# Second LayerNorm's scale and bias: spread over the partitions by TensorE from 16 columns, in place of a load into all partitions

## The chip, the cores and the metric

The kernel runs on one core of a Trainium2 chip. The metric is the device time of one execution in microseconds (us). The kernel before takes 1108.0 us as the median of three runs (1106.22 to 1109.04).

The core has five engines that take their instructions in order and meet at semaphores: TensorE (PE in the profile; its weight loads are the rows PEld), VectorE (DVE), ScalarE (ACT), GpSimd (POOL) and SyncE (SP), which here issues nearly all transfers. SBUF is the on-chip memory of 128 partitions, PSUM holds the matmul results.

## The reference, cut to what matters

One layer of a decoder with 256 tokens of 1024 features, all float32: four kinds of token mixer, a LayerNorm, a mixture of 32 experts of which each token takes four, and a second LayerNorm. The change concerns only the scale `ln2_g` and the bias `ln2_b` of the last line, 1024 numbers each, the same for all tokens.

```python
mix = token_mixers(x, ...)
x = _layernorm(DEEPNORM_ALPHA * x + mix, ln1_g[l], ln1_b[l])
ffn = moe_ffn(x, router_w[l], router_b[l], w_gu[l], b_gu[l], w_down[l], b_down[l])
x = _layernorm(DEEPNORM_ALPHA * x + ffn, ln2_g[l], ln2_b[l])

def _layernorm(x, g, b):
    mu = jnp.mean(xf, axis=-1, keepdims=True)
    var = jnp.mean(jnp.square(xf - mu), axis=-1, keepdims=True)
    y = (xf - mu) * lax.rsqrt(var + LN_EPS)
    return (y * g + b)
```

## The kernel before, in words

The front part (projections, attention, convolution, first LayerNorm, router) takes about the first 195 us. The rest is a loop over 32 places. The experts are ranked by the number of their tokens, a table gives each place its rank, and each place works on one expert; places 29 to 31 (`TAIL` = 3) are run only if their expert has tokens at all, and their weights are only then loaded (`loads`, behind a test of the count). In the run shown, place 29 is worked on, and places 30 and 31 are not.

The weights of a place are 12 chunks of 1 MiB (128 partitions of 2048 float32): chunks 0 to 7 for the gate and up projection (`up`, L1085), chunks 8 to 11 for the down projection (`down`, L1141). SP issues them in order of use into a ring of 19 slots of that size (tiles `w`, `wx`, `res`), each as soon as the slot's former user has given it back (`released`). TensorE waits in `up` and `down` for the semaphore of each slot. For a place with at most 32 tokens TensorE runs 8 matmul records of 128x512 per chunk in `up` and 16 of 128x256 in `down`.

Between `up` and `down` of a place stand: `act` (VectorE and ScalarE: clamp, sigmoid, products, L1100 to L1109), then on TensorE what the place has to do for others (the gather of a later batch of tokens, the scatter of an earlier batch, L1235, the gates' transposes, L1224, and in place 17 `b_down`, L1254 and L1265), then `h_trans` (two transposes, L1118), ScalarE's copy of them (L1122), the bias of the next place (L1073) and `down`. Places share batches: places 25 to 28 (ranks 16, 20, 24 and 28) are one batch, and place 29 is the first of the last batch, so that in place 29 TensorE scatters the results of places 25 to 28 (L1235) between `up` and `h_trans`. The results of the last batch are scattered after the loop, and then the second LayerNorm and the output follow.

The scale and the bias of the second LayerNorm need every partition to hold the same 2048 numbers. They lie in one ring slot, `g2b2`: SP issues a transfer from one row of `rows`, read 128 times, into all partitions (L1507), after the loads of place 28 and ahead of those of place 29. VectorE waits for it at the end (L1532) and uses it in L1534 and L1540.

```python
for e in range(1, E - TAIL):
    load(e, expert(e))
released(X, g2b2_before)
X.dma_start(g2b2, A["rows"][1:2].to_broadcast([128, SLOT])).then_inc(slot_sem[id(g2b2)], 16)
loads(E - TAIL)
```

The order of the work on each engine is written out by hand in `program`, which is run once for each engine; `take` waits for a semaphore and counts it down.

Of the kernel before, what the change touches and what calls it, by code (L numbers as in the profile page):

```python
# [27 lines left out]
AF = mybir.ActivationFunctionType  # L28
OP = mybir.AluOpType
# [12 lines left out]
SLOT = 2048  # L42
# [14 lines left out]
def _cols(c):  # L57
    if len(c) == 2:
# [7 lines left out]


_STAY = [("ident", 128), ("ones", 128), ("strict", 128), ("iota", 128), ("krow", 32), ("kcol", 2), ("sigma", 32),
         ("rep", 128), ("qmask", 4), ("half", 1), ("g1", 8), ("b1", 8)]
_FIRST = [("tri", 128), ("tri1", 128), ("causal", 256), ("hmask", 2), ("fb", 4), ("rb", 32), ("lam", 128), ("dng", 1),  # L70
          ("cw", 62), ("cb", 2), ("clg", 2), ("clb", 2), ("rw", 256)]
PK, PKW = {}, []
# [32 lines left out]
def layout(x, rel_bias, w_in, forget_b, diff_lambda, diff_norm_g, conv_w, conv_b, conv_ln_g, conv_ln_b,  # L105
           w_out, ln1_g, ln1_b, router_w, router_b, w_gu, b_gu, w_down, b_down, ln2_g, ln2_b):
    f = np.float32
    A = {}
    A["xt"] = np.ascontiguousarray(x[0].T.reshape(8, 128, L).transpose(1, 0, 2))
    A["xs"] = np.ascontiguousarray(x[0].reshape(2, 128, D).transpose(1, 0, 2))  # L110
    for i, c in enumerate(CHUNKS):
        w = np.concatenate([w_in[0][:, o:o + n] for o, n in _cols(c)], axis=1)
        A[f"wi{i}"] = np.ascontiguousarray(w.reshape(8, 128, CW[i]).transpose(1, 0, 2)).reshape(128, 8 * CW[i])
    wo = w_out[0].reshape(4, 2, 128, D)[[1, 2, 3, 0]].transpose(0, 2, 1, 3)
    A["wo"] = np.ascontiguousarray(wo).reshape(4, 128, SLOT)


    we = np.empty((E, 12, 128, SLOT), f)
    we[:, 0:8].reshape(E, 8, 128, 4, 2, 256)[...] = (
        w_gu[0].reshape(E, 8, 128, 4, 256, 2).transpose(0, 1, 2, 3, 5, 4))  # L120
    we[:, 8:12].reshape(E, 2, 2, 128, 2, D)[...] = w_down[0].reshape(E, 2, 2, 2, 128, D).transpose(0, 3, 1, 4, 2, 5)
    A["we"] = we
    A["bg"] = np.ascontiguousarray(b_gu[0].reshape(E, 4, 256, 2).transpose(1, 0, 3, 2)).reshape(128, 512)
    A["bd"] = np.ascontiguousarray(b_down[0].reshape(E, 4, 256).transpose(1, 0, 2)).reshape(128, 256)
    A["rows"] = np.stack([np.concatenate([g[0], b[0]]) for g, b in ((ln1_g, ln1_b), (ln2_g, ln2_b))])
    i = np.arange(128)
    P = {}
    P["ident"] = (i[:, None] == i[None]).astype(f)
    P["tri"] = (i[:, None] <= i[None]).astype(f)
    P["strict"] = (i[:, None] < i[None]).astype(f)  # L130
    P["iota"] = np.broadcast_to(np.arange(1, 129, dtype=f), (128, 128))
    k = np.arange(L)
    P["causal"] = np.where(k[None] <= i[:, None] + 128, 0.0, NEG).astype(f)
    P["ones"] = P["tri1"] = np.ones((128, 128), f)
    e = np.arange(E)
    key = np.where(e < 1, 1e5, -e)
    P["krow"] = np.broadcast_to(key, (128, E))
    P["kcol"] = np.stack([key, e], axis=1)[i % E]
    P["sigma"] = np.broadcast_to(SIGMA, (128, E))
    P["rep"] = (i[:, None] % E == i[None] % E).astype(f)  # L140
    P["qmask"] = (i[:, None] // 32 == np.arange(4)[None]).astype(f)
    P["half"] = np.full((128, 1), -0.5)
    P["hmask"] = (i[:, None] // 64 == np.arange(2)[None]).astype(f)
    P["fb"] = np.broadcast_to(forget_b, (128, 4))
    P["rb"] = np.broadcast_to(router_b, (128, 32))
    P["lam"] = np.broadcast_to(diff_lambda.reshape(1, 128), (128, 128))
    P["dng"] = np.tile(diff_norm_g[0], 2)[:, None]
    P["cw"] = conv_w[0].T.reshape(2, 128, 31).transpose(1, 0, 2).reshape(128, 62)
    for n, a in (("cb", conv_b), ("clg", conv_ln_g), ("clb", conv_ln_b)):
        P[n] = a[0].reshape(2, 128).T  # L150
    P["g1"] = ln1_g[0].reshape(8, 128).T
    P["b1"] = ln1_b[0].reshape(8, 128).T
    P["rw"] = router_w[0].reshape(8, 128, 32).transpose(1, 0, 2).reshape(128, 256)
    for n, l in (("pk0", _STAY), ("pk1", _FIRST)):
        A[n] = np.ascontiguousarray(np.concatenate([np.asarray(P[m], f) for m, _ in l], axis=1))
    dist = i[:, None] + 128 - k[None]
    t5 = rel_bias[_buckets()[np.maximum(dist, 0)]]
    t5 = np.where((dist >= 0)[..., None], t5, f(NEG)).astype(f)
    A["t5"] = np.ascontiguousarray(t5.transpose(0, 2, 1))
    return A  # L160


def body(ctx, tc, nc, A, out):
# [746 lines left out]
    for e in range(E):  # L910
        for c in range(12):
            t, before = queue.pop(0)
            n_used[id(t)] += e > 0
            slots[e, c] = t, before, n_used[id(t)]
            queue.append((t, (e, c)))
            if (e, c) == (0, 3):
                queue.append((rest, "rest"))
        if e == E - TAIL - 1:

            g2b2, g2b2_before = queue.pop(0)  # L920
            n_used[id(g2b2)] += 1
            g2b2_n = n_used[id(g2b2)]

    def sem(name, n=None):
        if n is None:
# [5 lines left out]
    FREE, READY, READYA, HT = sem("free", 8), sem("ready", 8), sem("readya", 8), sem("ht", 8)  # L931

    REL, REL11 = sem("rel"), sem("rel11")
    GC, SG, HH, VV = sem("gc"), sem("sg"), sem("hh"), sem("vv")
    PP, PPX, PGR, PGRX, YX, GT, SQ = [sem(n) for n in ("pp", "ppx", "pgr", "pgrx", "yx", "gt", "sq")]
    SEL, ACC, FIN, RS, RSD, OUT, DONE = [sem(n) for n in ("sel", "acc", "fin", "rs", "rsd", "out", "done")]

    def take(X, s, n=1):
        X.wait_ge(s, n).then_inc(s, -n)  # L939
# [21 lines left out]
    def program(X, kind):  # L961
# [309 lines left out]
        def one_hot_x(e, b):  # L1271
# [3 lines left out]
                                    op0=OP.add, op1=OP.is_equal)  # L1275
            return j

        def gather_x(e, b=0):

            if t_ and (b == 0 and HOME[e] == 4):  # L1280
                take(X, PPX)
            if HOME[e] + 4 * b < NPASS[e] and not s_:
                with more(e, HOME[e] + 4 * b):
                    if v_ and (b or HOME[e] < 4):
                        one_hot_x(e, b).then_inc(PPX)
                    if t_ and (b or HOME[e] < 4):
                        take(X, PPX)
                    for k0 in (0, 4):
                        gather(Px, XGx[b], k0, 6 + k0 // 4)
                    gather_x(e, b + 1)  # L1290
# [70 lines left out]
        def passes(e, end):  # L1361
# [42 lines left out]
            if not many:  # L1404
                scatter_before(e)
                gates_of(e)
                gather_next(e, 0)
                if h < 4:
                    gather_next(e, 4)
                if four(e + 1):  # L1410
                    gather_x(e + 1)
                if e == B_DOWN:
                    b_down()
            h_trans(e, 0)
            if not many and h == 4 and t_:
                take(X, PGRX)
# [20 lines left out]
            if many:  # L1437
                if e + 1 < E:
                    bias(e + 1, 0)
                gates_xT(e)  # L1440
                for k0 in (0, 4):
                    gather_next(e, k0)
                scatter_x(e)
                if four(e + 1):
                    gates_x(e + 1, 0)
                    gather_x(e + 1)
                if e == B_DOWN:
                    b_down()

        def places(first):  # L1450

# [36 lines left out]
        if kind == "SP":  # L1488
            def load(e, x, cs=range(12)):
                for c in cs:  # L1490
                    t, before, _ = slots[e, c]
                    released(X, before)
                    X.dma_start(t, A["we"][ds(x, 1), c].rearrange("o p n -> p (o n)")).then_inc(slot_sem[id(t)], 16)

            def expert(e):
                return X.value_load(eid[:, e:e + 1], min_val=0, max_val=E - 1)

            def loads(e):
                with X.If(X.value_load(cnt[:, e:e + 1], min_val=0, max_val=L) > 0):
                    load(e, expert(e))  # L1500
                    if e + 1 < E:
                        loads(e + 1)

            for e in range(1, E - TAIL):
                load(e, expert(e))
            released(X, g2b2_before)
            X.dma_start(g2b2, A["rows"][1:2].to_broadcast([128, SLOT])).then_inc(slot_sem[id(g2b2)], 16)  # L1507
            loads(E - TAIL)


# [18 lines left out]

        pieces = [(0, 0, D), (1, 0, D // 2), (1, D // 2, D)]  # L1530
        if v_:
            X.wait_ge(slot_sem[id(g2b2)], 16 * g2b2_n)  # L1532
            for tb in range(2):
                X.scalar_tensor_tensor(acc[:, tb], acc[:, tb], mv[:, tb, 0:1], g2, op0=OP.subtract, op1=OP.mult)  # L1534
                X.drain()  # L1535
                X.wait_ge(RSD, tb + 1)
                for t, c0, c1 in pieces:
                    if t == tb:
                        o = acc[:, tb, c0:c1]
                        X.scalar_tensor_tensor(o, o, mv[:, tb, 1:2], b2[:, c0:c1], op0=OP.mult, op1=OP.add).then_inc(OUT)  # L1540
# [43 lines left out]
```

## Time and profile before

| what | value |
|---|---|
| three runs, median (lowest to highest) | 1108.0 us (1106.22 to 1109.04) |
| profiled execution, its own time | 1105.45 us |
| its span, first to last instruction | 1103.7 us |
| TensorE busy | 925.4 us, 84% of the span |
| VectorE, ScalarE, GpSimd busy | 368.1, 173.5, 111.6 us |
| moved by DMA | 403.84 MB, mean 366 GB/s |
| mean granted TensorE clock | 0.904 |

The profiled execution is 2.55 us (0.23%) under the median of the runs. Its time is 1.75 us longer than its span. TensorE's busy share contains stretches at a lower clock, and it is an average over a front part that computes and a loop that mostly waits for weights; which of the two ends last in a stretch is read from that stretch.

### The profile page before, as it was taken

To read this page: it belongs to the slowest core of one execution; us is meant where nothing else is said; L and a number is where in the kernel's file an instruction comes from. 1 tells how busy PE (TensorE), PEld (TensorE's weight loads), DVE (VectorE), ACT (ScalarE), POOL (GpSimd) and SP (SyncE) were. 2 spreads that over 40 slices of the span, in tenths; PEclk is the share of its full clock that TensorE was granted. 3 is DMA by queue.
4 is the path that set the end of the run, shared out by engine and by line. 5 is a ranking of instruction groups with operands and counts; after the bars stand their busy time and mean duration, and the time that the engine had idled before them with its cause. 6 is when DMAs were issued, how large, how long until landed. Compare 5 with 4: busy or idle time off the path is not lost. (4 is left out here: it accounts for less than half of the span.)

```text
span 1103.7 us, 21204 instructions
## 1 busy us (share of the span) xinstructions
PE 925.4 (84%) x8340; PEld 479.9 (43%) x8340; DVE 368.1 (33%) x896; ACT 173.5 (16%) x371; POOL 111.6 (10%) x98
## 2 busy tenths in 40 slices
PE   9887898997799979877799986678999999776672
PEld 8786685453232536322245542132554544322121
DVE  4899655332113223211132331111332333211014
ACT  5525440210001201100011110000110111100000
POOL 2695613000000000000000000000000000000000
PEclk9898898999799999977899998779999999978667
DMA  9635356899999649999999999999999999999981
GB/s 372 247 140 204 115 201 281 355 377 427 426 426 425 245 185 424 425 427 427 425 426 425 425 426 426 426 426 426 425 426 424 425 426 425 425 426 427 426 375 46
DMA packets 57002, 403.84 MB, mean 366 GB/s; under 512 B 6320, under 2 KB 6448, under 8 KB 8368
## 3 DMA queue, kind: packets, MB, share of 16 engines
q1 hardware_dynamic: 56592, 400.98, 87.1%
q8 instruction: 84, 1.38, 0.5%
q10 hardware_dynamic: 288, 1.18, 0.3%
q14 instruction: 38, 0.31, 0.1%
HBM read 401.08 MB, written 1.05 MB: 364 GB/s over the span
## 5 line engine op out<-in xcount | busy, mean ns | idle before, releaser
L1085 PE MATMUL moe<-w,XG 128*32 128x512 f32 x2672 | 354.3, 658 | 84.8 <-DMA w<-in_we_dram 83.0
L1085 PEld LDWEIGHTS moe<-w,XG 128*32 128x32 f32 x2672 | 81.3, 114 | 325.5 <-DMA w<-in_we_dram 186.3
L1141 PE MATMUL moe<-w,hT 128*32 128x256 f32 x2880 | 174.9, 392 | 14.9 <-DMA w<-in_we_dram 10.5
L1100 DVE TENSOR_SCALAR gc<-moe 128x256 f32<-128x256 f32 x49 | 20.8, 425 | 418.3 <-DVEq L939 418.3
L1141 PEld LDWEIGHTS moe<-w,hT 128*32 128x32 f32 x2880 | 95.7, 113 | 88.2 <-issue 22.8
L1109 ACT ACTIVATE h<-gc 128x256 f32<-128x256 f32 x49 | 20.4, 416 | 490.7 <-ACTq L939 490.7
L1486 POOL CAST sel<-sel_q 128x128 fp32r<-128x128 f32 x31 | 9.3, 304 | 821.4 <-PE moe L1085 821.4
L1160 DVE COPY ys<-moe 32x256 f32<-32x256 f32 x94 | 39.5, 421 | 155.1 <-DVEq L939 154.0
L1160 ACT ACTIVATE ys<-moe 32x256 f32<-32x256 f32 x94 | 35.2, 374 | 184.4 <-ACTq L939 183.8
L858 PEld LDWEIGHTS moe<-P,z 128*128 128x128 f32 x448 | 56.7, 207 | 15.6 <-issue 15.5
L858 PE MATMUL moe<-P,z 128*128 128x128 f32 x448 | 60.6, 295 | 0.6 <-PEq L939 0.6
L1235 PE MATMUL moe<-ys,pgT 128*128 128x256 f32 x224 | 54.2, 387 | 4.7 <-PEq L939 3.0
L864 DVE TENSOR_SCALAR XG<-moe,pk 128x128 f32<-128x128 f32 x112 | 38.3, 405 | 50.5 <-DVEq L939 50.0
L262 PE MATMUL pj<-s,h 128*128 128x256 f32 (+1 forms) x272 | 51.5, 292 | 2.1 <-ACT sv L316 2.1
L1235 PEld LDWEIGHTS moe<-ys,pgT 128*128 128x128 f32 x224 | 40.4, 190 | 19.6 <-issue 15.3
L262 PEld LDWEIGHTS pj<-s,h 128*128 128x128 f32 (+1 forms) x272 | 43.6, 196 | 2.9 <-ACT sv L316 2.4
L1073 PE MATMUL moe<-bg,sel 128*128 128x512 f32 x100 | 38.3, 466 | 5.4 <-PEq L939 5.3
L1242 DVE TENSOR_TENSOR acc<-acc,moe 128x512 f32<-128x512 f32 x60 | 39.0, 684 | 9.6 <-DVEq L939 9.3
L262 PE MATMUL pj<-s,l 128*128 128x256 f32 (+1 forms) x136 | 39.5, 290 | 0.7 <-DVE l L279 0.7
L279 POOL TENSOR_TENSOR l<-w,h 128x2048 fp32r<-128x2048 f32 x5 | 30.2, 6068 | 15.4 <-ACT h L274 15.4
L1118 PE MATMUL moe<-pk,h 128*128 128x128 f32 x98 | 21.3, 302 | 12.1 <-PEq L939 12.1
L274 ACT ACTIVATE h<-w 128x2048 fp32r<-128x2048 f32 (+1 forms) x15 | 27.2, 1829 | 4.9 <-DVE l L279 3.4
(284 smaller groups left out, 854.0 us busy)
## 6 DMA issues: line engine op xcount, KB each, us to landing
w<-in_we_dram SPq DMA_DIRECT2D x323, 1024.0 KB, 26.2
wx<-in_we_dram SPq DMA_DIRECT2D x19, 1024.0 KB, 26.6
res<-in_we_dram SPq DMA_DIRECT2D x18, 1024.0 KB, 26.4
w<-in_wi_dram SPq DMA_DIRECT2D x11, 1024.0 KB, 17.3
w<-in_wo_dram SPq DMA_DIRECT2D x4, 1024.0 KB, 5.9
xt<-in_xt_dram SPq DMA_DIRECT2D x4, 256.0 KB, 4.9
w<-in_wi_dram SPq DMA_DIRECT2D x4, 256.0 KB, 5.0
t<-in_t_dram SPq DMA_DIRECT2D x1, 1024.0 KB, 15.6
```

Source lines behind the costliest of these rows:

```text
L262: T.matmul(o, R(l[x]), R(r[y]), start=first and i == 0, stop=last and i == 2)
L274: S.activation(R(view(hi[c][0], c)), view(tiles[c], c), AF.Copy)
L279: eng.tensor_tensor(R(W[c][1]), view(tiles[c], c), W[c][0], op=OP.subtract)
L858: i = X.matmul(p[:, a], z[:, tb, k * 128:k * 128 + 128], P[:, tb], start=tb == 0, stop=tb == 1)
L864: i = X.tensor_scalar(XG[:, k], p[:, a], par("g1")[:, k:k + 1], par("b1")[:, k:k + 1], op0=OP.mult, op1=OP.add)
L1073: X.matmul(pb_[b], R(sels[e % 3]), R(w), start=i == 0, stop=False, skip_group_check=True)
L1085: i = X.matmul(gu[32 * q:32 * q + 32], xg(e, p, k), w[:, q], start=False, stop=k == 7, skip_group_check=True)
L1118: i = X.transpose(q[:, j], hs[p % 2][:, j * 128:j * 128 + 128], ident)
L1141: i = X.matmul(y[o:o + 32], hT8[:, p, j, 32 * q:32 * q + 32], w[:, n * 256:n * 256 + 256], start=(j == 0 and q == 0), stop=(j == 1 and q = ...
L1160: i = X.tensor_copy(dst[o:o + 32, c], y[o:o + 32]) if v_ else X.activation(dst[o:o + 32, c], y[o:o + 32], AF.Copy)
L1235: i = X.matmul(p[:, n * 256:n * 256 + 256], g[:, 2 * (2 * m + n) + tb], y[:, 2 * m + n], start=True, stop=True, skip_group_check=True)
L1242: X.tensor_tensor(o, o, p, op=OP.add).then_inc(FREE[b], 2)
```

## The change

The 2048 numbers come in as 16 columns of a parameter tile (`gb2`: column k holds 128 of them, one on each partition), with the transfer that loads the tile anyway: that one grows from 727 to 743 columns. The transfer of `g2b2` from `rows` is gone, and the slot is still taken out of the ring. A new function `rows2` fills it in place 28, in four rounds of 512 numbers: VectorE multiplies the identity by four of the columns (a 128x512 tile `PGx`, four diagonals), TensorE multiplies a matrix of ones by that tile (each row of the result holds the 512 numbers), and ScalarE copies the result from PSUM into the slot. VectorE may write the next diagonals when ScalarE has seen the matmul end (`DF`). VectorE's wait before the last LayerNorm is for `GB`, which ScalarE raises after the fourth copy.

```diff
-         ("rep", 128), ("qmask", 4), ("half", 1), ("g1", 8), ("b1", 8)]
+         ("rep", 128), ("qmask", 4), ("half", 1), ("g1", 8), ("b1", 8), ("gb2", 16)]
...
-    A["rows"] = np.stack([np.concatenate([g[0], b[0]]) for g, b in ((ln1_g, ln1_b), (ln2_g, ln2_b))])
+    A["rows"] = np.concatenate([ln1_g[0], ln1_b[0]])[None]
...
+    P["gb2"] = np.concatenate([ln2_g[0].reshape(8, 128), ln2_b[0].reshape(8, 128)]).T
...
             g2b2, g2b2_before = queue.pop(0)
-            n_used[id(g2b2)] += 1
-            g2b2_n = n_used[id(g2b2)]
...
+    DD, DF, GB = sem("dd"), sem("df"), sem("gb")
...
+        def rows2():
+
+            if s_:
+                released(X, g2b2_before)
+            for r in range(4):
+                b = 5 + r % 3
+                if v_:
+                    if r:
+                        take(X, DF)
+                    X.tensor_tensor(PGx.rearrange("p t r a b -> p (t r) (a b)"), ident[:, None].to_broadcast([128, 4, 128]),
+                                    par("gb2")[:, 4 * r:4 * r + 4, None].to_broadcast([128, 4, 128]), op=OP.mult).then_inc(DD)
+                if t_:
+                    take(X, DD)
+                    take(X, FREE[b], 2)
+                    X.matmul(pb_[b], par("ones"), PGx.rearrange("p t r a b -> p (t r a b)"), start=True,
+                             stop=True).then_inc(READYA[b])
+                if s_:
+                    take(X, READYA[b])
+                    if r < 3:
+                        X.sem_inc(DF, 1)
+                    X.activation(g2b2[:, 512 * r:512 * r + 512], pb_[b], AF.Copy).then_inc(FREE[b], 2)
+            if s_:
+                X.drain().then_inc(GB)
...
                 if e == B_DOWN:
                     b_down()
+                if e == E - TAIL - 1:
+                    rows2()
             h_trans(e, 0)
...
-            released(X, g2b2_before)
-            X.dma_start(g2b2, A["rows"][1:2].to_broadcast([128, SLOT])).then_inc(slot_sem[id(g2b2)], 16)
             loads(E - TAIL)
...
-            X.wait_ge(slot_sem[id(g2b2)], 16 * g2b2_n)
+            X.wait_ge(GB, 1)
```

The call of `rows2` stands a second time in the form of place 28 for more than 32 tokens, which the run shown does not take.

TensorE's instructions of place 28 before: the last chunks of `up` (L1085), the two transposes (L1118), the bias of place 29 (L1073), `down` (L1141).

```order
L1085 MATMUL moe<-w_1027,XG_1585 32x512 x4
L1085 MATMUL moe<-w_1029,XG_1585 32x512 x4
L1118 MATMUL moe<-pk_66,h_1595 128x128 x2
L1073 MATMUL moe<-bg_67,sel_1600 128x512
L1073 MATMUL moe<-bg_68,sel_1600 128x512
L1141 MATMUL moe<-w_1152,hT_1576 32x256 x8
L1141 MATMUL moe<-res_1317,hT_1576 32x256 x8
```

The same place after; L1292 is the new matmul (`PGx` the diagonals, `pk` the tile with the matrix of ones).

```order
L1085 MATMUL moe<-w_1027,XG_1585 32x512 x4
L1085 MATMUL moe<-w_1029,XG_1585 32x512 x4
L1292 MATMUL moe<-PGx,pk_66 128x512 x4
L1118 MATMUL moe<-pk_66,h_1595 128x128 x2
L1073 MATMUL moe<-bg_67,sel_1600 128x512
L1073 MATMUL moe<-bg_68,sel_1600 128x512
L1141 MATMUL moe<-w_1152,hT_1576 32x256 x8
```

The four matmuls stand between the last chunk of `up` and the transposes, and everything of TensorE behind them keeps its order.

ScalarE's instructions of the same place after: the sigmoid (L1109), the four new copies into the slot (L1298, tile `w_1158`), the copy of the transposes (L1122), its half of the results of `down` (L1160).

```order
L977 COMPARE_AND_BRANCH
L1109 ACTIVATE h_1595<-gc 128x256
L1298 ACTIVATE w_1158<-moe 128x512 x4
L1122 ACTIVATE hT_1576<-moe 128x256
L1160 ACTIVATE ys<-moe 32x256 x2
```

Before, L1122 follows L1109 at once; VectorE has its four products (128x512) at the same place, behind the product that ends `act` (L1106).

SP's transfers before, from the last two chunks of place 28 to the first of place 29.

```order
L1493 DMA w_1154<-in_we_dram 128x2048
L1493 ISA
L1493 DMA w_1156<-in_we_dram 128x2048
L1507 DMA w_1158<-in_rows_dram 128x2048
L1499 TENSOR_LOAD cnt
L1499 ISA x2
L1499 COMPARE_AND_BRANCH
L1496 TENSOR_LOAD eid
L1496 ISA x2
L1493 ISA
L1493 DMA w_1434<-in_we_dram 128x2048
```

After, the row with `in_rows_dram` is missing, and no other row of SP's moves.

## Rows read from the trace of the kernel before

**Rows 1.** The page: bandwidth in 40 slices of the span, wait for weights in `up`, transfers

```profile
GB/s 372 247 140 204 115 201 281 355 377 427 426 426 425 245 185 424 425 427 427 425 426 425 425 426 426 426 426 426 425 426 424 425 426 425 425 426 427 426 375 46
...
L1085 PE MATMUL moe<-w,XG 128*32 128x512 f32 x2672 | 354.3, 658 | 84.8 <-DMA w<-in_we_dram 83.0
...
w<-in_we_dram SPq DMA_DIRECT2D x323, 1024.0 KB, 26.2
```

**Rows 2.** Stretches: from:to, its length, busy us of each engine, PEclk, DMA share, GB/s

```profile
1018.00:1037.40 19.40, 13.02 (x64) 1.48 (x64) 0.74 (x2) 0.59 (x2) 0.29 (x1) 0.68 1.01 426
1037.40:1047.00 9.60, 6.04 (x68) 2.88 (x68) 2.09 (x6) 1.37 (x4) 0.00 (x0) 0.71 1.01 428
...
1050.00:1062.00 12.00, 8.61 (x40) 0.92 (x40) 0.00 (x0) 0.00 (x0) 0.00 (x0) 0.64 1.01 427
1062.00:1070.30 8.30, 5.73 (x24) 0.60 (x24) 0.00 (x0) 0.00 (x0) 0.00 (x0) 0.50 0.91 385
1070.30:1083.00 12.70, 9.81 (x99) 7.29 (x96) 4.95 (x10) 2.52 (x6) 0.00 (x0) 1.00 0.28 118
```

**Rows 3.** Timeline of places 28 and 29, all engines: start, length, instruction, idle before and releaser

```profile
1018.27 6.17 SPq L1507 DMA_DIRECT2D w<-in_rows_dram  x1
...
1039.46 0.42 DVE L1106 TENSOR_TENSOR h<-h,moe 128x256 f32<-128x256 f32 x1 [0.51 <-DVEq L939]
...
1040.02 0.66 PE L1118 MATMUL moe<-pk,h 128*128 128x128 f32 x2 [2.69 <-PEq L939]
...
1040.82 0.38 ACT L1122 ACTIVATE hT<-moe 128x256 f32<-128x256 f32 x1 [2.24 <-ACTq L939]
...
1045.22 1.07 PE L1141 MATMUL moe<-w,hT 128*32 128x256 f32 x16 [0.22 <-DMA w<-in_we_dram]
...
1050.08 1.93 PE L1085 MATMUL moe<-w,XG 128*32 128x512 f32 x8 [3.80 <-DMA w<-in_we_dram]
...
1059.90 1.82 PE L1085 MATMUL moe<-w,XG 128*32 128x512 f32 x8 [1.28 <-DMA w<-in_we_dram]
...
1063.57 1.94 PE L1085 MATMUL moe<-w,XG 128*32 128x512 f32 x8 [1.86 <-DMA w<-in_we_dram]
...
1066.01 1.93 PE L1085 MATMUL moe<-w,XG 128*32 128x512 f32 x8 [0.50 <-DMA w<-in_we_dram]
...
1068.44 1.94 PE L1085 MATMUL moe<-w,XG 128*32 128x512 f32 x8 [0.50 <-DMA w<-in_we_dram]
...
1070.31 4.10 PE L1235 MATMUL moe<-ys,pgT 128*128 128x256 f32 x16
```

**Rows 4.** Lines by form, whole span: nearest forms to the new copy and product

```profile
L1228 ACT ACTIVATE pgT<-moe 128x512 f32<-128x512 f32 x28 | 15.3, 595 | 44.0 <-ACTq L939 44.0
...
L258 DVE TENSOR_TENSOR s<-xt,s 128x1024 fp32r<-128x1024 f32 x2 | 2.4, 1224 | 8.2 <-ACT s L257 8.2
```

**Rows 5.** Timeline of place 17 around its `b_down`: VectorE's last product, then TensorE

```profile
710.74 0.42 DVE L1106 TENSOR_TENSOR h<-h,moe 128x256 f32<-128x256 f32 x1
...
720.96 0.69 PE L1118 MATMUL moe<-pk,h 128*128 128x128 f32 x2
...
722.43 1.94 PE L1141 MATMUL moe<-res,hT 128*32 128x256 f32 x16
724.14 3.47 PE L1141 MATMUL moe<-w,hT 128*32 128x256 f32 x48
727.61 5.36 PE L1085 MATMUL moe<-w,XG 128*32 128x512 f32 x48
734.34 1.07 PE L1085 MATMUL moe<-w,XG 128*32 128x512 f32 x8 [1.37 <-DMA w<-in_we_dram]
736.77 1.06 PE L1085 MATMUL moe<-w,XG 128*32 128x512 f32 x8 [1.37 <-DMA w<-in_we_dram]
```

**Rows 6.** Timeline of an earlier batch change, TensorE

```profile
946.90 1.06 PE L1085 MATMUL moe<-res,XG 128*32 128x512 f32 x8 [1.38 <-DMA res<-in_we_dram]
947.89 4.10 PE L1235 MATMUL moe<-ys,pgT 128*128 128x256 f32 x16
```

More of the change, by code (lines that the diff above doesn't have):

```diff
@@ L1448, in passes @@
                     b_down()
+                if e == E - TAIL - 1:
+                    rows2()
         def places(first):
```

## The prediction

> **What bounds the kernel now.** First the page's bandwidth line [rows 1]: from about the tenth slice nearly every slice stands at 424 to 427 GB/s, two stretches apart, until the last but one; and TensorE's matmuls of `up` have 84.8 us of idle time before them, 83.0 of it put down to transfers of weights. So in the loop the transfers set the pace, although TensorE is the busiest engine. Then the stretches around places 28 and 29 [rows 2]: 426 to 428 GB/s at a DMA share of 1.01 up to 1062 us, so no byte can arrive earlier there unless another byte goes. Then the timeline [rows 3]. TensorE starts the last chunk of place 28 at 1045.22, just after it came (0.22 us idle), and the first chunk of place 29 at 1050.08, after 3.80 us idle. That is 4.86 us for two transfers, the one of the LayerNorm's rows (SP issued it at 1018.27) and chunk 0 of place 29: 2.43 us each. Chunk 7 starts at 1068.44 (0.50 us idle before it, for its transfer). From there TensorE waits for no transfer any more: the scatter of the last full batch follows at 1070.31, then `down`, the last scatter, the LayerNorm and the output. I take 1070.31 to the end of the span at 1103.7 (33.4 us) as a fixed tail, and ask when its first instruction can start.
>
> **The removed transfer.** One transfer of 1 MiB leaves a saturated queue. All 12 chunks of place 29 come behind it, so each lands one step earlier: 2.43 us from the timeline [rows 3]; 1.049 MB at 427 GB/s [rows 2] is 2.46, the same. Chunk 7 is then there at 1068.44 - 2.43 = 1066.01. SP's issue of the removed transfer took 6.17 us [rows 3], but a transfer of weights lands 26.2 us after its issue in the median [rows 1], so some ten are queued, and the issue itself sets nothing. The ring slot is still taken, and no load of place 29 needs a slot that is given back later than chunk 5 of place 28, which TensorE reads before the new work. The new work can therefore not hold up a load. This term: -2.43 us. The 16 columns in the parameter tile are 8 KB, 0.02 us at 427 GB/s, in the front part; the test of `GB` in place of the slot's semaphore costs nothing, since the slot is full by about 1053 and read only behind the scatter of 1070.31.
>
> The Trainium skill ("DMA: Bandwidth & Descriptors", section "Where 436 GB/s comes from") says that for loads from HBM the HBM side binds at about 358 GB/s per core. By that page 1.049 MB would be an estimated 2.93 us, and the forecast 0.5 us lower. The rows measure 427 GB/s, and the measurement decides.
>
> **The added work.** In place 28 the last product of `act` ends at 1039.46 + 0.42 = 1039.88, and TensorE starts the transposes 0.14 us later, at 1040.02 [rows 3]. Now four rounds stand between them, each a chain of VectorE, TensorE, ScalarE and back. No row shows these forms, so by the nearest:
> - the product of 128x512 on VectorE: half of the 1.224 us of 128x1024 is 0.61 [rows 4]; I take 0.65.
> - the matmul: the trace gives two records for each float32 matmul, and 16 records of 256 columns take 4.10 us in the scatter at the full clock of 1.00 [rows 2, 3], 0.256 each. Two records of 512 columns are 4 x 0.256 = 1.03 us at 2.4 GHz, and twice that, 2.05, at 1.2 GHz.
> - a hand-over from engine to engine: 0.14 (VectorE to TensorE, above; TensorE to ScalarE too, 1040.02 + 0.66 to 1040.82 [rows 3]). Three per round, since VectorE's next product waits until ScalarE has seen the matmul end.
> - ScalarE's copy, 0.595 [rows 4], lies beside the next product. The fourth one stands ahead of ScalarE's copy of the transposes: up to 0.3 us.
>
> One round is 0.65 + 1.03 + 3 x 0.14 = 2.10 us at the full clock and 3.12 at half. The first matmul can start at 1040.67 and the transposes after three rounds and one matmul: 1040.67 + 6.30 + 1.03 = 1048.0, or 1040.67 + 9.36 + 2.05 = 1052.1. So TensorE is held 8.0 to 12.1 us, the largest cost of the change. Queued behind it are the transposes, the bias of place 29 and `down` of place 28; ScalarE's and VectorE's parts of the results of `down` wait with them. VectorE and ScalarE have nothing else to do there (2.09 and 1.37 us busy in 9.6 [rows 2]).
>
> **What hides it.** Place 17 shows the same thing with `b_down` [rows 5]: the last product ends at 711.16 and the transposes start at 720.96, a hold of 9.8 us with TensorE at half clock (0.69 us for two transposes). From there 6.65 us pass until `up` of the next place starts at 727.61. Its first six chunks had come meanwhile and are done in 5.36 us, 0.89 each. By 734.34 TensorE waits for a transfer again. With these two durations `up` of place 29 starts between 1048.0 + 6.65 = 1054.7 and 1052.1 + 6.65 = 1058.7, plus up to 0.3. Six chunks later it is 1060.0 to 1064.4. Chunk 6 lands at 1066.01 - 2.43 = 1063.58 and is done by 1065.3 at the latest, and chunk 7 comes at 1066.01. TensorE has caught up 0.7 us before it or more. If `up` started later than 1066.01 - 7 x 0.89 = 1059.8, the delay would begin to show one to one.
>
> **The clock behind it.** In place 29 the clock was low before (0.64, then 0.50 [rows 2]) and chunk 7 took 1.94 us, so the scatter started 1.87 us after it [rows 3]. After catching up, TensorE was at the full clock: in place 17 the two chunks behind the dense stretch take 1.07 and 1.06 us [rows 5], and where a batch change followed one, the scatter starts 0.99 us after the last chunk of 1.06 [rows 6]. I expect this for place 29 too, which gives 0.88 us more.
>
> **The sum**, against the profiled execution: 1105.45 - 2.43 - 0.88 = 1102.1 us. That execution is 2.55 us under the median of the runs, so the forecast for a median is 1108.0 - 3.31 = 1104.7 us.
>
> **Rivals.**
> 1. Only the transfer counts: TensorE has fallen back to 1.2 GHz by chunk 7, or chunks 8 to 11 come so late that `down` waits. 1105.45 - 2.43 = 1103.0, as a median 1105.6. For it: with waits between the chunks the clock does fall (0.68, 0.64 [rows 2]). Against: the first two chunks after catching up were fast in place 17.
> 2. The time is given back: place 29 lands no earlier. For it: chunk 5 of place 29 came 3.67 us after chunk 4 (1059.90 to 1063.57 [rows 3]), 1.24 more than a step, while the share fell to 0.91 and the rate to 385 GB/s [rows 2]; something other than the bytes in the queue held it, and could take the rest too. Against: the step of the removed transfer is there to be seen at full rate. Price: 0, a median of 1108.0.
> 3. Slower: TensorE stays at 1.2 GHz from the first round through `up` of place 29. Transposes at 1052.1; 1.47 us later `down` (720.96 to 722.43 [rows 5]), four chunks at 1.71 (722.43 to 724.14), so `up` from 1060.4; eight chunks at 2 x 0.89 = 1.79 end at 1074.7, 4.4 us after 1070.31. 1109.9, as a median 1112.4. It decides when `up` starts at half clock later than 1070.31 - 14.3 = 1056.0. Against: in place 17 the first chunk of `down` took 1.94, but the next three together 3.47, and then 0.89 per chunk: back to back work brought the clock up.
>
> The Trainium skill speaks for the third ("TensorE: Matmul & The Clock Gate", section "HAM oscillation — how this bites in real kernels"): bursts of matmuls between waits can each start throttled, over and over. By that rule alone the four rounds and what follows run at half clock and the third rival's time comes out. Place 17 agrees with the throttled start and not with its lasting.
>
> **How the numbers follow.** Forecast 0.52, first rival 0.22, second 0.12, third 0.10, and 0.04 for still larger gains. A median of three scatters by an estimated 1.2 us, since the runs shown reach from 1.8 under to 1.0 over theirs. What a measurement of this kernel can tell from no change is about 0.3%, 3.3 us: below 1104.7 is faster, above 1111.3 slower. The forecast lies on that edge and gives half of its chance to faster (0.26), the first rival a third (0.07), the second 0.02, the rest 0.03: 0.38. Slower: 0.08 of the third rival and 0.02 of mishaps in the others: 0.10. Same: 0.52. The forecast's own range is 1103.4 to 1106.0. The range reaches down to 1101.8, for runs as quick as the profiled execution, and up to 1109.2, the second rival with its scatter; beyond it lie the third rival and little else.
>
> **What would show it.** In the profile after: no transfer from `rows`; four matmul pairs in place 28 with 2 to 3 us between their starts; the transposes of place 28 between 1048 and 1053; hardly a wait before the first chunks of place 29 and a wait for a transfer before its chunk 7, which starts near 1066.0 and takes 1.07; the scatter at about 1067.0 and the tail behind it 33.4 us long, as before. A chunk 7 of 1.9 us means the first rival; one that starts at 1068 after a wait, the second; one without a wait before it, after 1066, the third. A tail of another length would make the argument wrong where I looked least.

## The result, and the profile after

The change made the kernel slower: 1116.58 us as the median of four runs (1115.9 to 1119.42) against 1108.3 us of four runs before. The recorded ratio is 1.0095, with a 95% interval of 1.0069 to 1.0121; the plain quotient of the two medians is 1.0075, inside that interval. The forecast was 1104.7 us, 3.6 us faster by this median of before; the result lies above the range.

The first view to read is the page's line of bandwidth, in 40 slices of the span, of the kernel after.

```profile
GB/s 366 248 128 213 113 200 300 343 381 421 420 420 420 244 181 419 420 421 420 420 420 419 419 420 420 421 421 419 419 420 417 420 420 418 421 420 421 420 366 45
```

Before, the slices of the loop stand at 424 to 427 [rows 1]; now they stand at 417 to 421, from the tenth slice on, that is from about 250 us, some 800 us ahead of the place that was changed. The stretches of the kernel after say the same (from:to, length, busy us of PE, PEld, DVE, ACT and POOL, PEclk, DMA share, GB/s); the single line below them is the kernel before:

```profile
420.00:520.00 100.00, 81.07 (x779) 37.17 (x777) 24.50 (x64) 10.05 (x25) 1.45 (x5) 0.89 1.01 420
...
640.00:760.00 120.00, 88.38 (x702) 36.68 (x700) 25.61 (x70) 8.70 (x22) 1.20 (x4) 0.82 1.01 420
...
860.00:962.00 102.00, 98.78 (x1043) 47.47 (x1036) 31.71 (x81) 13.23 (x33) 0.94 (x3) 0.98 1.01 419
```

```profile
860.00:962.00 102.00, 95.50 (x1040) 49.31 (x1036) 34.12 (x85) 14.91 (x37) 0.94 (x3) 1.00 1.01 425
```

The DMA share is 1.01 in both kernels: the queues are as full as before, and fewer bytes come through in the same time. The next view is the timeline of places 28 and 29 after (start, length, engine, line, instruction, idle before and releaser).

```profile
1029.92 1.94 PE L1085 MATMUL moe<-w,XG 128*32 128x512 f32 x8 [1.41 <-DMA w<-in_we_dram]
...
1051.38 0.42 DVE L1106 TENSOR_TENSOR h<-h,moe 128x256 f32<-128x256 f32 x1 [0.51 <-DVEq L939]
1051.72 0.68 DVE L1287 TENSOR_TENSOR PGx<-pk 128x512 f32<-128x512 f32 x1
...
1052.71 2.05 PE L1292 MATMUL moe<-PGx,pk 128*128 128x512 f32 x2 [3.45 <-PEq L939]
1054.98 0.60 ACT L1298 ACTIVATE w<-moe 128x512 f32<-128x512 f32 x1 [4.49 <-ACTq L939]
1055.05 0.69 DVE L1287 TENSOR_TENSOR PGx<-pk 128x512 f32<-128x512 f32 x1 [2.64 <-DVEq L939]
...
1056.03 2.05 PE L1292 MATMUL moe<-PGx,pk 128*128 128x512 f32 x2 [1.28 <-PEq L939]
...
1062.65 2.04 PE L1292 MATMUL moe<-PGx,pk 128*128 128x512 f32 x2 [1.26 <-PEq L939]
...
1064.49 0.64 PE L1118 MATMUL moe<-pk,h 128*128 128x128 f32 x2
...
1066.16 1.62 PE L1141 MATMUL moe<-w,hT 128*32 128x256 f32 x16 [0.18 <-PEq L939]
...
1071.21 6.22 PE L1085 MATMUL moe<-w,XG 128*32 128x512 f32 x56 [0.84 <-issue]
...
1078.45 1.06 PE L1085 MATMUL moe<-w,XG 128*32 128x512 f32 x8 [1.02 <-DMA w<-in_we_dram]
1079.45 4.10 PE L1235 MATMUL moe<-ys,pgT 128*128 128x256 f32 x16
```

The first chunk of place 28 in the kernel before:

```profile
1018.21 1.49 PE L1085 MATMUL moe<-w,XG 128*32 128x512 f32 x8 [0.50 <-DMA w<-in_we_dram]
```

The reader is to compare two distances, not the absolute times. The first chunk of place 28 starts at 1029.92; before, it was 1018.21, so 11.71 us are lost ahead of all the new instructions. From there to the scatter of place 29 it is 49.53 us; before, it was 52.10 (1018.21 to 1070.31 [rows 3]), so 2.57 us are won in the stretch that was changed. From the scatter to the end of the span it is 34.65 us against 33.39. The three add up: 11.71 - 2.57 + 1.26 = 10.4, which is the difference of the spans of the two profiled executions (1114.1 and 1103.7); the medians of all runs differ by 8.3.

The theory to be tested: the 16 columns lengthen a tile that is allocated ahead of the ring. In the built program the 18 slots of the ring's pool begin at byte 18176 + 8192 i of each partition before and at 18240 + 8192 i after; the nineteenth, `wx`, begins at 173824 and 173888. 18176 is 71 x 256, and 18240 is 64 bytes past it. By the theory, transfers into such slots are slower. The rivals: the arrays in HBM, the memory that the weights come from (`rows` is half as long, `pk0` wider), or the new code.

### The profile page after: what moved, and what is told of

It is laid out like the page before. It is cut to its first block, busy times and chain, and to the rows that moved or that the text cites. A ratio compares the mean times of both kernels' runs of the same rounds, so it can differ in the third digit from the quotient of the medians.

```text
span 1114.1 us, 21246 instructions
## 1 busy us (share of the span) xinstructions
PE 927.5 (83%) x8348; PEld 482.5 (43%) x8348; DVE 371.0 (33%) x900; ACT 176.0 (16%) x375; POOL 111.6 (10%) x98
## 5 line engine op out<-in xcount | busy, mean ns | idle before, releaser
L1085 PE MATMUL moe<-w,XG 128*32 128x512 f32 x2672 | 348.4, 650 | 79.8 <-DMA w<-in_we_dram 77.4
L1085 PEld LDWEIGHTS moe<-w,XG 128*32 128x32 f32 x2672 | 81.5, 113 | 313.6 <-DMA w<-in_we_dram 168.3
L1141 PE MATMUL moe<-w,hT 128*32 128x256 f32 x2880 | 173.1, 388 | 19.1 <-DMA w<-in_we_dram 11.7
L1141 PEld LDWEIGHTS moe<-w,hT 128*32 128x32 f32 x2880 | 95.5, 112 | 91.6 <-issue 24.8
L1109 ACT ACTIVATE h<-gc 128x256 f32<-128x256 f32 x49 | 20.4, 417 | 482.5 <-ACTq L939 482.5
L1160 DVE COPY ys<-moe 32x256 f32<-32x256 f32 x94 | 39.5, 421 | 156.8 <-DVEq L939 155.7
L1160 ACT ACTIVATE ys<-moe 32x256 f32<-32x256 f32 x94 | 35.3, 375 | 185.1 <-ACTq L939 184.5
L1235 PE MATMUL moe<-ys,pgT 128*128 128x256 f32 x224 | 56.8, 402 | 5.3 <-PEq L939 3.9
L1235 PEld LDWEIGHTS moe<-ys,pgT 128*128 128x128 f32 x224 | 42.8, 200 | 21.1 <-issue 15.8
L1073 PE MATMUL moe<-bg,sel 128*128 128x512 f32 x100 | 38.6, 469 | 5.5 <-PEq L939 5.3
L1118 PE MATMUL moe<-pk,h 128*128 128x128 f32 x98 | 20.8, 295 | 9.0 <-PEq L939 9.0
```

Source lines behind the costliest of these rows:

```text
L1073: X.matmul(pb_[b], R(sels[e % 3]), R(w), start=i == 0, stop=False, skip_group_check=True)
L1085: i = X.matmul(gu[32 * q:32 * q + 32], xg(e, p, k), w[:, q], start=False, stop=k == 7, skip_group_check=True)
L1141: i = X.matmul(y[o:o + 32], hT8[:, p, j, 32 * q:32 * q + 32], w[:, n * 256:n * 256 + 256], start=(j == 0 and q == 0), stop=(j == 1 and q = ...
L1160: i = X.tensor_copy(dst[o:o + 32, c], y[o:o + 32]) if v_ else X.activation(dst[o:o + 32, c], y[o:o + 32], AF.Copy)
L1235: i = X.matmul(p[:, n * 256:n * 256 + 256], g[:, 2 * (2 * m + n) + tb], y[:, 2 * m + n], start=True, stop=True, skip_group_check=True)
```

## The experiments

Each is timed against the kernel before on the same chip, and each ratio is the recorded one. The runs of one kernel spread by 4.5 to 12.8 us, so where a few us matter the distances in the timeline carry the verdict, of one profiled execution each.

**The slots moved, nothing else.** The kernel before with an unused tile of 64 bytes per partition.

```diff
     pk = [pk_p.tile([128, PKW[0]], F32, name="pk0")]
+    gap = pk_p.tile([128, 16], F32, name="gap")
```

> The kernel before, with 64 unused bytes per partition allocated behind the parameter tile, so that the 18 ring slots begin at byte 18240 of each partition in place of 18176 (71 x 256); the arrays in HBM, the transfers and the code are those of before. Theory of the address: transfers into slots that do not begin at a multiple of 256 bytes run at 420 GB/s in the loop in place of 426; about 11 us (1.0%) slower than before, 1117 to 1121 us. Rival of the code or of the HBM arrays (rows halved, pk0 wider): as before, 1108 us and 426 GB/s.

Measured: 1118.99 us against 1108.26, ratio 1.0101 (1.0053 to 1.0149). The bandwidth line:

```profile
GB/s 371 239 143 196 113 198 301 342 396 421 420 419 420 214 173 420 420 420 422 420 420 419 419 419 421 420 421 420 418 419 419 419 419 419 420 421 421 420 359 44
```

The whole loss is there with the code, the transfers and the HBM arrays of before. Both rivals fall.

**The change without the move.** The 16 columns as a tile of their own, allocated late, loaded from an array of their own on ScalarE's queue.

```diff
-         ("rep", 128), ("qmask", 4), ("half", 1), ("g1", 8), ("b1", 8), ("gb2", 16)]
+         ("rep", 128), ("qmask", 4), ("half", 1), ("g1", 8), ("b1", 8)]
...
     cnt = mo.tile([1, E], I32, name="cnt")
+    gb2 = one("gb2", 16)
+    nc.scalar.dma_start(gb2, A["gb2"])
...
```

> The changed kernel, but the 16 columns are a small tile of their own, allocated late and loaded on ScalarE's queue, so that the parameter tile and all ring slots lie where they lay before (18176). Theory of the address: 426 GB/s in the loop, and the local gain of the change is left: 1104 to 1107 us, 1 to 4 us faster than before. Rival of the code (new instructions, longer program) or of the halved array of rows: 420 GB/s and about 1116 us.

Measured: 1105.2 us against 1108.26, ratio 0.9983 (0.9955 to 1.0011). The bandwidth line, and three rows of TensorE's timeline (line numbers are shifted by 2: L1087 is `up`, L1237 the scatter):

```profile
GB/s 363 258 119 226 115 202 298 352 373 426 427 426 425 232 176 425 425 427 426 426 425 425 426 425 426 426 426 427 424 426 423 425 426 424 426 426 427 427 373 47
```

```profile
1018.67 1.07 PE L1087 MATMUL moe<-w,XG 128*32 128x512 f32 x8 [1.41 <-DMA w<-in_we_dram]
...
1059.36 6.22 PE L1087 MATMUL moe<-w,XG 128*32 128x512 f32 x56 [0.82 <-issue]
1066.62 1.07 PE L1087 MATMUL moe<-w,XG 128*32 128x512 f32 x8 [1.04 <-DMA w<-in_we_dram]
1067.62 4.10 PE L1237 MATMUL moe<-ys,pgT 128*128 128x256 f32 x16
```

The rate of before is back. From the first chunk of place 28 to the scatter it is 48.95 us, 3.15 less than before. In the whole time the interval still holds 1, so faster is likely here and not shown.

**The change with the slots at another multiple of 256.** As changed, with 192 unused bytes more, so that the slots begin at 18432 = 72 x 256; one small early tile (`lt`) shares a place to make room.

```diff
+    gap = pk_p.tile([128, 48], F32, name="gap")
...
-    lt = fp.tile([128, 2, 32], F32, name="lt")
+    lt = fp.tile([128, 2, 32], F32, name="lt", tag="k2")
```

> The changed kernel with its 16 columns in the parameter tile, and 192 more unused bytes behind it, so that the slots begin at 18432 (72 x 256); one small early tile shares another's place to make room. Theory of the address: 426 GB/s, 1104 to 1107 us, as the kernel with the tile of its own. Rival that any move of the slots, or the wider array in HBM, costs: 420 GB/s and 1116 us.

Measured: 1104.93 us against 1108.26, ratio 0.9972 (0.9948 to 0.9996): against before 3 us faster, with an interval that only just leaves out 1. 423 to 427 GB/s in the loop; the distance from place 28 to the scatter is 48.85 us (L1086 is `up`, L1236 the scatter):

```profile
1021.69 1.06 PE L1086 MATMUL moe<-w,XG 128*32 128x512 f32 x8 [1.51 <-DMA w<-in_we_dram]
...
1069.54 1.06 PE L1086 MATMUL moe<-w,XG 128*32 128x512 f32 x8 [1.04 <-DMA w<-in_we_dram]
1070.54 4.10 PE L1236 MATMUL moe<-ys,pgT 128*128 128x256 f32 x16
```

So the wider array in HBM and the move as such do not cost the 11 us. This is the version to keep.

**The slots moved by 128 bytes.** The kernel before with a gap of 32 columns, and `lt` as above.

> The kernel before, with the slots moved by 128 bytes to 18304 (a multiple of 128, not of 256). If multiples of 256 are what counts: 420 GB/s and 1117 to 1121 us, as with 64 bytes. If multiples of 128 or 64 are enough in some measure: between, down to 1108 us and 426 GB/s. Rival of code or HBM arrays: 1108 us.

Measured: 1118.4 us against 1108.26, ratio 1.0108 (1.0063 to 1.0153), 419 to 421 GB/s. A multiple of 128 is not enough.

**Half of the slots moved.** The gap of 64 bytes between the ninth and the tenth slot.

```diff
+    gaps = []
...
         if t is None:
+            if i == 9 and not gaps:
+                gaps.append(ring.tile([128, 16], F32, name="gap", tag="gap"))
```

> The kernel before with the 64 unused bytes between the ninth and the tenth slot: nine of the 19 slots begin at multiples of 256, ten do not, and all tiles behind them are moved as well. If the destination address of each transfer is what costs, ten nineteenths of the loss: about 423 GB/s in the loop and 5 to 6 us more than before, 1113 to 1115 us. Rival that the moved tiles of the other engines cost (they are all moved here): about 420 GB/s and the whole 11 us. Rival that a threshold on the whole ring decides: 426 or 420, nothing between.

Measured: 1111.02 us against 1106.43, ratio 1.0023 (1.0 to 1.0047), and:

```profile
GB/s 370 245 137 205 113 200 268 367 369 425 426 423 424 230 181 425 422 426 425 423 426 422 424 423 425 426 424 425 423 423 423 423 424 424 425 425 426 425 343 43
```

Between: the rate stands at 422 to 426 GB/s, so the other engines' tiles (all of them behind the gap were moved) do not carry the whole loss, and no threshold on the whole ring decides. But it is less than the share of ten nineteenths would give (5 to 6 us were expected): a miss, which the last set takes up.

**The removed transfer by itself.** The kernel before without the load of the rows, and nothing in its place: the last LayerNorm takes other numbers that lie in SBUF, so its scale and bias are left out.

```diff
-            released(X, g2b2_before)
-            X.dma_start(g2b2, A["rows"][1:2].to_broadcast([128, SLOT])).then_inc(slot_sem[id(g2b2)], 16)
...
-            X.wait_ge(slot_sem[id(g2b2)], 16 * g2b2_n)
...
-        g2, b2 = g2b2[:, 0:D], g2b2[:, D:]
+        g2, b2 = [t.rearrange("p k n -> p (k n)") for t in XGs]
```

> The kernel before without the transfer of the LayerNorm's rows and with nothing in its place; the last LayerNorm takes other numbers that lie in SBUF (this leaves the scale and bias out). It shows the removed transfer by itself. By the prediction chunk 7 of place 29 starts 2.4 us earlier, counted from the first chunk of place 28 (47.8 us after it in place of 50.2), still at half clock or so, so the scatter follows 1.9 us behind it: 2 to 3 us faster than before, 1105 to 1106 us. If the added work costs nothing, the same time as the kernel with the tile of its own, or up to 0.9 us more for the clock. Rival that the added work costs some us: clearly faster than that kernel, 1101 to 1103 us.

Measured: 1102.77 us against 1106.43, ratio 0.9971 (0.9947 to 0.9995). TensorE's timeline:

```profile
1021.78 1.07 PE L1085 MATMUL moe<-w,XG 128*32 128x512 f32 x8 [1.36 <-DMA w<-in_we_dram]
...
1064.78 1.94 PE L1085 MATMUL moe<-w,XG 128*32 128x512 f32 x8 [1.65 <-DMA w<-in_we_dram]
1067.22 1.71 PE L1085 MATMUL moe<-w,XG 128*32 128x512 f32 x8 [0.51 <-DMA w<-in_we_dram]
1069.65 1.07 PE L1085 MATMUL moe<-w,XG 128*32 128x512 f32 x8 [0.72 <-DMA w<-in_we_dram]
1070.65 4.10 PE L1235 MATMUL moe<-ys,pgT 128*128 128x256 f32 x16
```

Chunk 7 starts 47.87 us after the first chunk of place 28 (before 50.23): 2.36 us earlier, the price of the transfer. With the added work it is 47.95 in the kernel with the tile of its own and 47.85 in the one with the slots at 18432. So the added work is hidden to 0.1 us at this point. The whole time does not settle this: 1102.77 lies in the range that was named for a costly added work, but the kernel before was quicker too in this set, and the intervals of the ratios overlap (0.9971 here, 0.9983 and 0.9972 with the work). Against the expectation, chunk 7 ran at the full clock here too, with no dense stretch ahead of it; chunks 5 and 6 did not.

**The added work twice over.** The kernel with the tile of its own, and eight rounds in place of four.

```diff
-            for r in range(4):
-                b = 5 + r % 3
+            for i in range(8):
+                b, r = 5 + i % 3, i % 4
...
```

> The kernel with the tile of its own, and the four rounds run twice over (the second pass writes the same numbers again): TensorE is held some 13 us longer in place 28. In the single form TensorE has caught up 1.0 us before chunk 7 of place 29 lands, so by the prediction's cover 12 of the 13 us must now show: scatter of place 29 about 61 us after the first chunk of place 28 in place of 49, 1116 to 1118 us in all, and no wait before chunk 7. Rival that TensorE's time in this stretch is always hidden: 1105 us.

Measured: 1118.05 us against 1106.43, ratio 1.008 (1.0047 to 1.0113).

```profile
1022.95 1.94 PE L1087 MATMUL moe<-w,XG 128*32 128x512 f32 x8 [1.37 <-DMA w<-in_we_dram]
...
1067.77 2.04 PE L1294 MATMUL moe<-PGx,pk 128*128 128x512 f32 x2 [1.26 <-PEq L941]
1069.61 0.63 PE L1120 MATMUL moe<-pk,h 128*128 128x128 f32 x2
...
1076.53 7.07 PE L1087 MATMUL moe<-w,XG 128*32 128x512 f32 x64 [0.85 <-issue]
1083.54 4.09 PE L1237 MATMUL moe<-ys,pgT 128*128 128x256 f32 x16
```

All eight chunks of place 29 run without a wait between them, and the scatter comes 60.59 us after the first chunk of place 28, 11.6 later than with four rounds. The cover is real and it was nearly used up: 13.2 us more of work show as 11.6.

**The dose.** Three kernels, with one run each: the gap behind the third slot (16 of 19 slots moved), behind the fourteenth (5 of 19), and all slots moved by 32 bytes.

> As the kernel with half of the slots moved, but with the 64 bytes behind the third slot: 16 of 19 slots do not begin at a multiple of 256. Rows of the transfers from 640 to 1000 us are compared: with all slots moved a row of 8 KB takes 315.9 ns on its DMA engine, with none 311.0, with ten of 19 312.2. If every transfer to a moved slot costs the same and the ten were a matter of chance: 315.1 ns, 421 GB/s. If a moved row costs only where a neighbouring transfer is moved too (the share squared): 314.4 ns or less, 421 to 422 GB/s.

> The 64 bytes behind the fourteenth slot: 5 of 19 slots do not begin at a multiple of 256. Same cost for each transfer to a moved slot: 312.3 ns a row, 424 GB/s. Cost only beside another moved one (share squared): 311.3 ns, 425 GB/s, hardly to be told from none.

> The kernel before with all slots moved by 32 bytes. If only a multiple of 256 is free of loss and the distance from one does not matter (64 and 128 bytes cost the same): 316 ns a row, 420 GB/s, 1115 to 1122 us. If a smaller step costs less: between 311 and 316 ns.

Measured: 1115.8, 1104.42 and 1118.39 us, against 1103.59 of the kernel before, one run each. What is compared is the mean duration of the transfer records of 8 KB (one partition's row of a chunk) that start from 640 to 1000 us of the span, worked out from each trace, with the share of them that took 309 ns, the shortest there is, and the bandwidth of that stretch. The expectations have 311.0, 312.2 and 315.9 ns, some 1.1 ns more than here: those means also held 29 longer records of 16 KB from another queue.

| slots not at a multiple of 256 | ns a row | rows at 309 ns | GB/s | share of the loss |
|---|---|---|---|---|
| none (before) | 309.96 | 99.7% | 425 | 0 |
| 5 of 19 (0.26) | 310.00 | 98.5% | 426 | 0.01 |
| 10 of 19 (0.53) | 311.05 | 78.8% | 424 | 0.23 |
| 16 of 19 (0.84) | 313.39 | 31.9% | 421 | 0.73 |
| all, by 64 bytes | 314.66 | 7.4% | 420 | 1 |
| all, by 128 bytes | 314.31 | 32.1% | 420 | 0.92 |
| all, by 32 bytes | 315.54 | 6.9% | 418 | 1.19 |
| all (the changed kernel) | 314.63 | 7.4% | 420 | 0.99 |

The four other kernels with every slot at a multiple of 256 (the two repaired ones, the one without the load, the one with the work twice over) give 309.96 or 309.97, so the steps of the table are clear of the noise. A same cost for each moved row does not fit (0.26, 0.53 and 0.84 were wanted). The square of the share (0.07, 0.28, 0.71) comes near at the two larger ones and is too high for the smallest. The column of 309 ns shows it row by row: with ten of 19 slots moved, 79% of the rows are as quick as before, while only nine slots of 19 (47%) stayed where they were. The slots are used in turn, so some three rows in ten went to a moved slot at no extra time. In order of time the slow rows of that kernel come in groups, with few between them, and the pattern returns every 19 chunks, one round of the ring. So a moved row's time depends on the transfers around it; how, no run here shows. With 5 of 19 slots moved all other tiles behind them were moved too, at 0.01 of the loss, so those tiles do not carry it. The smallest step, 32 bytes, costs most.

## Why the prediction was wrong

**The step that failed** is the one sentence on the parameter tile: "The 16 columns in the parameter tile are 8 KB, 0.02 us at 427 GB/s, in the front part". It priced the columns as bytes that are moved. Their price was the place they take: 64 bytes per partition ahead of the ring. That moved the destination of every weight transfer off its multiple of 256, and the rate of the loop, which the sum took as given (427 GB/s), became 420. The 11.71 us lost over the 336 chunks up to place 28 are 0.035 us each; the table's 4.67 ns a row, with eight rows of a chunk on each of the 16 DMA engines, are an estimated 0.037. The kernel with nothing but the move shows it, and the changed kernel without the move does not. Counted from the first matmul of `up`, the loop up to place 28 takes 835.6 to 838.7 us in the kernel before and the four others with every slot at a multiple of 256, and 846.9 to 849.6 in the four with every slot moved. None of the rivals was this mechanism: the third gave a loss too (1112.4 us) by another one, TensorE at half clock through place 29, and the seven chunks done in 6.22 us in the kernel after rule that out.

The Trainium skill has a rule that bears on it ("DMA: Bandwidth & Descriptors", section "How a descriptor splits into AXI transactions"): a transaction has to start at a multiple of 256 bytes, so a transfer that does not start there begins with one that fetches bytes it does not use, and they cost beats of 32 bytes all the same. The page tells this of what is read; here it is the address written to that lies off the multiple. By its count of beats a row of 8192 bytes that starts 64 bytes late has 258 in place of 256, an estimated 0.8%; the traces have 1.5% a row (309.96 to 314.63 ns). By the same count 32 bytes would cost an estimated 0.4% and 128 bytes 1.6%; the traces have 1.8% and 1.4%. That there is a loss agrees; its size and its order do not.

**The removed transfer, -2.43 us**: right. 2.36 us with the transfer alone gone.

**The added work, a hold of 8.0 to 12.1 us on TensorE**: right in its mechanism and a little short in size. In the kernel after, the transposes start 12.69 us after the last product (1051.80 to 1064.49, with 0.14 of it there before), so the hold is 12.55 us, 0.5 over the upper end. The terms: product 0.69 (0.65 was taken), matmul 2.05 at half clock, as written, copy 0.60. The rounds are 3.31 us apart in place of 3.12, because the hand-overs of a round take 0.57 us together (0.29, 0.21 and 0.06) and not 0.42. TensorE was at half clock in all four rounds.

**What hides it**: right, with less to spare than it sounds. `up` of place 29 started 6.72 us after the transposes (6.65 from place 17), seven chunks took 6.22 (7 x 0.89), and TensorE waited 1.0 us for chunk 7 (0.7 or more was written). With eight rounds the delay showed nearly one to one.

**The clock behind it, -0.88 us**: the number came out in the three kernels with the added work (scatter 1.00 us behind chunk 7), but it is not shown to be the work's doing. Of the eight kernels without that work, chunk 7 took 1.06 or 1.07 us in three (the one without the load, and those with the gap behind the third and the fourteenth slot), 1.53 in one and 1.94 in four, before among them. So the sum counted as a gain of the change what other executions without it have too, and how much of the 0.88 us is the work's is open.

**The sum.** With the slots at a multiple of 256 again the change gives 1104.93 us (1104.7 was forecast), and 3.15 to 3.25 us less from place 28 to the scatter (3.31). That this comes so near is in part luck, since 0.88 of it is the clock of chunk 7 in the one trace of before; up to the start of chunk 7 the gain is 2.3 to 2.4 us, the removed transfer alone. The tail, from that scatter to the end of the span, was taken as fixed and is not: 33.39 us before, 34.65 after, 34.08 and 35.06 in the two repaired kernels, but also 33.59 to 35.54 in the six kernels in which only slots were moved and the code is that of before. So its growth is not shown to come from the change; why it varies was not tried.

## What to carry to other kernels

A tile's size is a cost also for whatever is allocated behind it. Before a few columns are added to a tile, look at where the buffers of the big transfers begin in the two builds, and keep them at multiples of 256 bytes: a late tile of its own or some padding was worth over 11 us here, more than three times what the change itself brought. And when a result contradicts a local argument, look first at where in the span the two traces part: here it was 800 us ahead of the changed code.

## What the runs showed of the hardware that was not expected

- Rows of 8 KB from HBM into SBUF took 310.0 ns in the mean when all destinations began at a multiple of 256 bytes, and 314.3 to 315.5 ns when all lay 32, 64 or 128 bytes past one; the core's rate went from 425 or 426 to 418 to 420 GB/s.
- With 5 of 19 slots moved the loss was 1% of the whole, with 10 of 19 it was 23%: rows to a moved slot can take as little as rows to the others, and the loss grows faster than the share of moved slots.
- Slots from 18176 and from 18432 on are equally good, 309.96 ns a row (both multiples of 256, one of 512).
